# Experts' weights in tiles of 128 by 4096 (16 KB per partition) in five raw buffers, instead of tiles of 128 by 2048 in nine

## Chip, core and metric

The kernel runs on one core of a Trainium2 chip. The metric is device microseconds (us) of one execution, the median of several. Engines are named as the profile names them: PE is TensorE (PEld its weight load), DVE is VectorE, ACT is ScalarE, POOL is GpSimd, and SP is SyncE, which here issues almost all DMAs.

## What is computed

Two layers of a decoder trunk for 256 tokens of width 1024, in float32. Each layer has four token mixers, gates and an output projection, and then a feed-forward part: dense SwiGLU in layer 0, and in layer 1 eight experts, of which each token takes the best two. The change concerns the experts:

```python
def moe_swiglu(h, w_router, w1, w3, w2):        # w1, w3: 8 x 1024 x 3584, w2: 8 x 3584 x 1024
    logits = jnp.dot(t, w_router)
    top_val, top_idx = lax.top_k(logits, TOP_K)
    ...
    for e in range(N_EXPERTS):
        out = out + combine[:, e:e + 1] * swiglu(t, w1[e], w3[e], w2[e])
```

## The kernel before

**Weights.** All weights, 105 tiles of the mixers and the dense part and 336 of the experts, come from HBM in tiles of 1 MB, 128 partitions by 2048 floats. `load_raw` takes a buffer of 8 KB per partition, named `raw`, from a ring and issues the DMA on SP's queue; the ring is in the program's order, so a DMA waits on SP until the tile that had its buffer has been read for the last time, and all later DMAs wait behind it. In the front (mixers and dense part) the ring has four buffers (`rawp`); for the experts five more are put ahead of them (`rawm`), nine in all. `load_w` splits a tile for exact products: for each half of it, 1024 floats per partition, ACT copies it to `whi` (rounded, L165) and DVE computes `wlo = raw - whi` (L166). There are six pairs of `whi` and `wlo`. `mm3` makes a product from three matmuls: hi by hi (L157), hi by lo (L158), lo by hi (L159).

**Experts.** The eight experts are ordered by their tokens and paired: a large one with 128 slots, whose weights are split, and a small one with 64 slots, which reads `raw` itself with plain float32 matmuls, w1 on one half of PE's columns and w3 on the other. The 3584 hidden columns are done in seven chunks of 512, so there are 4 pairs x 7 = 28 steps. `paired` staggers them. In step s PE makes, in this order:

- `psu` of the large expert's chunk s (`up_large`, w1 and then w3: 48 matmuls), and between them `psT` (`turn_large`, four transposes);
- `psds`, the small expert's down projection of chunk s-2 (`down_small`: 16 matmuls straight from `raw`);
- `psq`, its up projection of chunk s-1 (`up_small`: 32 matmuls straight from `raw`), whose result ACT and DVE turn into `gfs` (L934, L935);
- `psd`, the large expert's down projection of chunk s-1 (`down_large`: 24 matmuls from split weights), and `psTs` (`turn_small`, four transposes of `gfs`).

So a step reads 12 tiles: w1, w1, w3, w3 of the large expert, w2, w2 of the small one, its w1, w3, w1, w3, and w2, w2 of the large one. At a change of pair PE also gathers the next pair's tokens (`psg`, `psgt`) and adds the results of the old one to the tokens (`pssc`).

The order on each engine is made by a scheduler when the program is built and is fixed after that. ACT and DVE work strictly in that order: an instruction that waits holds up all behind it.

Of the kernel before, what the change touches and what calls it, by code (L numbers as in the profile page):

```python
# [10 lines left out]
F32 = mybir.dt.float32  # L11
F32R = mybir.dt.float32r
# [5 lines left out]
P = 128  # L18
# [10 lines left out]
CONV_K = 31  # L29
WINDOWS = (2, 4, 8, 16)  # L30
NSLOT = 128
NRAW = 4
NRAW_MOE = 5
NSMALL = 64
RMS_EPS = 1e-6
LN_EPS = 1e-5
# [59 lines left out]
def decoder_kernel(ctx, tc, x_in, consts_in, mconsts_in, bias_in, small_in, gln_in, gbs_in, norms_in, w_in,  # L96
# [8 lines left out]
    psB = ctx.enter_context(tc.tile_pool(name="psB", bufs=4, space=bass.MemoryType.PSUM))  # L105


    ring = {"pools": [rawp] * NRAW, "i": 0, "skip": 0, "after": []}

    def hold_splits(ins, skip):  # L110

# [7 lines left out]
            yield  # L119

    def load_raw(src, a, n):
        pool = ring["pools"][ring["i"] % len(ring["pools"])]
        ring["i"] += 1
        raw = pool.tile([P, a, n], F32, name="raw", tag="raw")
        nc.sync.dma_start(raw, src)
        return raw

    def load_w(src, a, n):

        raw = load_raw(src, a, n)
        halves = []
        for i in range(2):
            r = raw[:, i * (a // 2):(i + 1) * (a // 2)]
            hi = wp.tile([P, a // 2, n], F32R, name="whi", tag="whi")
            lo = wp.tile([P, a // 2, n], F32R, name="wlo", tag="wlo")
# [4 lines left out]
        return halves, a // 2  # L142

    def wsl(wt, k, c0, n):
        halves, ah = wt
# [15 lines left out]
    def sl(pair, *idx):  # L161
        return (pair[0][idx], pair[1][idx])
# [505 lines left out]
    def moe(i, norm_i, l, mT):  # L668
        with ExitStack() as lctx:
# [6 lines left out]
            ring.update(pools=[rawm] * NRAW_MOE + [rawp] * NRAW, i=0)  # L676

            def small(shape, name, dt=F32):
                return wk.tile(shape, dt, name=name, tag=name, bufs=1)
# [129 lines left out]
            class Slots:  # L809
# [53 lines left out]

            line = {"last": []}

            def up_large(e, c, j0, xl):
                ps = psA.tile([P, 512], F32, name="psu", tag="mm")
                wt = [load_w(tile_of(e, c, j0 + j, 4), 4, 512) for j in range(2)]
                for k in range(KD):
                    last = mm3(ps, sl(xl, slice(None), k), wsl(wt[k // 4], k % 4, 0, 512), k == 0, k == KD - 1,  # L870
                               line["last"] if k == 0 else ())
                line["last"] = [last]
                return ps

            def gate_large(p1, p3):
                gf = wk.tile([P, 512], F32, name="gfm", tag="gf", bufs=2)
# [15 lines left out]
            def down_large(e, c, gT):  # L892
                if c == 0:
                    acc["l"] = [psB.tile([P, 512], F32, name=f"psd{n}", tag="ax") for n in range(2)]
                for j in range(2):
                    wt = load_w(tile_of(e, c, 4 + j, 2), 2, D)
                    for k in range(2):
                        for n in range(2):
                            last = mm3(acc["l"][n], sl(gT, slice(None), 2 * j + k), wsl(wt, k, n * 512, 512),
                                       c == 0 and j == 0 and k == 0, c == nch - 1 and j == 1 and k == 1,  # L900
                                       line["last"])
                            line["last"] = [last]

            def to_tokens(t, n, lhs, parts, w):
                ps = psA.tile([P, 512], F32, name="pssc", tag="mm")
# [15 lines left out]

            def up_small(e, c, xs):
                ps = psA.tile([P, 512], F32, name="psq", tag="mm")
                for j in range(2):
                    w1 = load_raw(tile_of(e, c, j, 4), 4, 512)
                    w3 = load_raw(tile_of(e, c, 2 + j, 4), 4, 512)
                    for k in range(4):
                        kk = 4 * j + k
                        for rows, w in ((LO, w1), (HI, w3)):
                            with behind(line["last"]):  # L930
                                line["last"] = [nc.tensor.matmul(ps[rows], lhsT=xs[:, kk], rhs=w[:, k], start=kk == 0,  # L931
                                                                 stop=kk == KD - 1)]
# [13 lines left out]
            def down_small(e, c, gT):  # L946
                if c == 0:
                    acc["s"] = psB.tile([P, 512], F32, name="psds", tag="ax")
                for j in range(2):
                    w = load_raw(tile_of(e, c, 4 + j, 2), 2, D)  # L950
                    for k in range(2):
                        for n, rows in enumerate((LO, HI)):
                            with behind(line["last"]):
                                line["last"] = [nc.tensor.matmul(  # L954
                                    acc["s"][rows], lhsT=gT[:, 2 * j + k], rhs=w[:, k, n * 512:(n + 1) * 512],
                                    start=c == 0 and j == 0 and k == 0, stop=c == nch - 1 and j == 1 and k == 1)]

            def scatter_small(GT, w):
                ys = wk.tile([P, 2, 512], F32R, name="ys", tag="ys", bufs=1)
# [5 lines left out]
            def paired():  # L965

                npair = NE // 2
                steps = npair * nch
                slots = {0: first}
                pend = gTs = None  # L970
                for s in range(steps + 1):
                    if s < steps:
                        pr, c = divmod(s, nch)
                        p1 = up_large(place_of[pr], c, 0, slots[pr].xl)
                    if pend is not None:
                        gT = turn_large(pend)
                    if s < steps:
                        gf = gate_large(p1, up_large(place_of[pr], c, 2, slots[pr].xl))
                        if c == nch - 1 and pr + 1 < npair:
                            nxt = slots[pr + 1] = Slots()  # L980
                            nxt.one_hot(None, posp[:, :, pr + 1:NE:npair])
                            nxt.inputs(0, NSLOT + NSMALL)
                            nxt.turned()
                    if s >= 2:
                        pr2, c2 = divmod(s - 2, nch)
                        down_small(place_of[npair + pr2], c2, gTs)
                        if c2 == nch - 1:
                            scatter_small(slots[pr2].GT, combp[:, :, npair + pr2:npair + pr2 + 1])
                    if s >= 1:
                        pr1, c1 = divmod(s - 1, nch)  # L990
                        gfs = up_small(place_of[npair + pr1], c1, slots[pr1].xs)
                        if s == steps:
                            sqrt_table(gfs[HI, 0:1], HI)
                        down_large(place_of[pr1], c1, gT)
                        if c1 == nch - 1:
                            scatter_large(slots[pr1].GT, combp[:, :, pr1:pr1 + 1])
                        gTs = turn_small(gfs)
                    pend = gf if s < steps else None
                down_small(place_of[NE - 1], nch - 1, gTs)
                scatter_small(slots[npair - 1].GT, combp[:, :, NE - 1:NE])  # L1000

            def rest(first_slot):
# [4 lines left out]
                for e in range(NE):  # L1007
# [4 lines left out]
                    sl_e.turned()  # L1012
                    for c in range(nch):
                        p1 = up_large(e, c, 0, sl_e.xl)
                        gT = turn_large(gate_large(p1, up_large(e, c, 2, sl_e.xl)))
                        down_large(e, c, gT)
                    scatter_large(sl_e.GT, comb[:, :, e:e + 1])

# [43 lines left out]
def layouts(inputs):  # L1062
# [5 lines left out]
    for l in range(L):  # L1068
# [13 lines left out]
    tiles = [f[k].reshape(M, NE, 2, 4, P, nch, 512).transpose(0, 1, 5, 2, 4, 3, 6).reshape(M, NE, nch, 2, P, 2048)  # L1082
             for k in ("moe_w1", "moe_w3")]
    tiles.append(f["moe_w2"].reshape(M, NE, nch, 2, 2, P, D).transpose(0, 1, 2, 3, 5, 4, 6)
                 .reshape(M, NE, nch, 2, P, 2048))
# [28 lines left out]
```

## Time and profile before

| | |
|---|---|
| median of 3 runs | 1543.84 us (1541.98 to 1545.42) |
| profiled execution | 1544.51 us, of which the span of the instructions is 1542.8 us |
| PE, DVE, ACT busy | 96%, 64%, 52% of the span |
| HBM read | 472.17 MB, 307 GB/s over the span |
| experts' part | from about 690 us to the end |

"Busy" of PE is modelled from overlapping matmuls, so a busy PE can still be a PE that is a little held up; how far apart matmuls start tells more. DMA share is the mean busy share of the 16 DMA engines. MB and GB/s are decimal, so a tile of 128 x 2048 floats is 1.05 MB.

### The profile page before, as it was taken

The numbers are of one execution on the slowest core, as the hardware profiler recorded it, in microseconds if no ns is written. First come the engines' busy times: TensorE is split into PE (matmuls) and PEld (weight loads), VectorE is DVE, ScalarE is ACT, GpSimd is POOL, SyncE is SP. The second block draws the span as 40 slices with busy tenths as digits, with TensorE's granted clock in tenths as the row PEclk, the third lists the DMA queues.
The fourth block names the chain that finished last, engine by engine and source line by source line (L and its number), as shares of the span: only waits on it lengthen the run. The fifth ranks groups of instructions, "written<-read, shape, count | busy, mean of one in ns | idle before, by whom it ended". The sixth has DMA issues, their size and how long they took to land.

```text
span 1542.8 us, 20057 instructions
## 1 busy us (share of the span) xinstructions
PE 1486.8 (96%) x7508; PEld 1072.2 (69%) x7508; DVE 979.9 (64%) x1291; ACT 809.6 (52%) x1184; POOL 20.3 (1%) x47
## 2 busy tenths in 40 slices
PE   6999998999989999989999999999999999899997
PEld 5888897888878888977566556656655665456553
DVE  5896776655668967756555565546654654556454
ACT  5567755555564777546454445435533553545343
POOL 2000000000000000000000000000000000000000
PEclk9999999999999999969999999999999999999998
DMA  9656455555555555639999999999999999999994
GB/s 333 192 178 201 162 191 170 191 188 186 178 193 178 177 181 164 265 125 383 385 421 421 421 394 420 421 421 421 421 405 421 421 421 421 375 397 421 421 421 199
DMA packets 134889, 474.61 MB, mean 308 GB/s; under 512 B 7744, under 2 KB 77376, under 8 KB 91776
## 3 DMA queue, kind: packets, MB, share of 16 engines
q1 hardware_dynamic: 132512, 466.65, 78.2%
q0 software_dynamic: 1984, 6.08, 1.2%
q8 instruction: 61, 1.00, 0.3%
q10 hardware_dynamic: 288, 0.52, 0.1%
q14 instruction: 44, 0.36, 0.1%
HBM read 472.17 MB, written 1.05 MB: 307 GB/s over the span
## 4 chain that ended last, share of the span: by engine, by line
PE 92%; DVE 4%; ACT 2%; issue 1%; DMA 1%; SPq 0%; DVEq 0%; ACTq 0%
PE psw L241 17%; PE psq L931 13%; PE psw L243 8%; PE psu L158 7%; PE psu L157 7%; PE psu L159 7%; PE psds L954 7%; PE psd L158 3%; PE psd L157 3%; PE psd L159 3%; DVE wlo L166 2%; PE psg L836 2%; PE psf L157 1%; PE psf L159 1%; PE psf L158 1%; PE psb L157 1%
## 5 line engine op out<-in xcount | busy, mean ns | idle before, releaser
L166 DVE TENSOR_TENSOR wlo<-raw,whi 128x1024 fp32r<-128x1024 f32 x546 | 648.3, 1222 | 242.0 <-ACT whi L165 237.9
L165 ACT ACTIVATE whi<-raw 128x1024 fp32r<-128x1024 f32 x546 | 554.6, 1054 | 272.8 <-DMA raw<-in_moe_w_dram 166.6
L241 PE MATMUL psw<-hp,whi 128*128 128x512 f32 x1088 | 388.7, 400 | 0.8 <-DVE hp L166 0.8
L243 PE MATMUL psw<-hp,wlo 128*128 128x256 f32 x1088 | 306.9, 282 | 0.0
L241 PEld LDWEIGHTS psw<-hp,whi 128*128 128x128 f32 x1088 | 205.0, 188 | 53.2 <-issue 3.3
L243 PEld LDWEIGHTS psw<-hp,wlo 128*128 128x128 f32 x1088 | 206.1, 189 | 2.1 <-issue 1.1
L931 PE MATMUL psq<-raw,xs 128*64 128x512 f32 x896 | 198.1, 593 | 1.8 <-DVE x L909 1.8
L157 PE MATMUL psu<-whi,xer 128*128 128x512 f32 x448 | 176.7, 394 | 3.2 <-DVE x L909 3.2
L158 PE MATMUL psu<-wlo,xer 128*128 128x512 f32 x448 | 177.8, 397 | 0.0
L159 PE MATMUL psu<-whi,xel 128*128 128x512 f32 x448 | 175.6, 392 | 0.0
L931 PEld LDWEIGHTS psq<-raw,xs 128*64 128x64 f32 x896 | 64.3, 137 | 129.0 <-issue 125.9
L954 PE MATMUL psds<-raw,gTs 128*64 128x512 f32 x448 | 103.6, 599 | 0.0
L157 PEld LDWEIGHTS psu<-whi,xer 128*128 128x128 f32 x448 | 84.8, 189 | 22.6 <-DVE x L909 4.5
L158 PEld LDWEIGHTS psu<-wlo,xer 128*128 128x128 f32 x448 | 84.8, 189 | 21.9 <-DVE wlo L166 3.7
L158 PE MATMUL psd<-wlo,gTr 128*128 128x512 f32 x224 | 92.2, 412 | 4.8 <-DVE wlo L166 4.8
L159 PEld LDWEIGHTS psu<-whi,xel 128*128 128x128 f32 x448 | 84.7, 189 | 16.9
L157 PE MATMUL psd<-whi,gTr 128*128 128x512 f32 x224 | 92.3, 412 | 2.7 <-ACT whi L165 2.7
L934 ACT ACTIVATE gfs<-psq 64x512 f32<-64x512 f32 x28 | 16.6, 591 | 143.2 <-PE psq L931 143.2
L935 DVE TENSOR_TENSOR gfs<-gfs,psq 64x512 f32<-64x512 f32 x28 | 19.4, 692 | 112.4 <-ACT gfs L934 112.4
L159 PE MATMUL psd<-whi,gTl 128*128 128x512 f32 x224 | 87.7, 391 | 0.0
L260 ACT ACTIVATE sum<-psw 128x256 f32<-128x256 f32 x120 | 44.8, 373 | 67.2 <-PE psw L243 67.2
L954 PEld LDWEIGHTS psds<-raw,gTs 128*64 128x64 f32 x448 | 29.8, 136 | 57.3 <-issue 56.3
(260 smaller groups left out, 1561.9 us busy)
## 6 DMA issues: line engine op xcount, KB each, us to landing
raw<-in_moe_w_dram SPq DMA_DIRECT2D x336, 1024.0 KB, 11.4
raw<-in_dense_w_dram SPq DMA_DIRECT2D x33, 1024.0 KB, 5.3
raw<-in_w_gate_dram SPq DMA_DIRECT2D x32, 1024.0 KB, 5.4
raw<-in_w_in_dram SPq DMA_DIRECT2D x22, 1024.0 KB, 5.5
raw<-in_w_out_dram SPq DMA_DIRECT2D x8, 1024.0 KB, 5.0
raw<-in_w_br_c_dram SPq DMA_DIRECT2D x4, 1024.0 KB, 5.3
s<-in_bias_dram POOLq DMA_DIRECT2D x16, 192.0 KB, 4.1
gain<-in_norms_dram SPq DMA_DIRECT2D x5, 512.0 KB, 4.6
```

The source lines that it names most:

```text
L157: nc.tensor.matmul(ps, lhsT=lhs[0], rhs=rhs[0], start=start, stop=False)
L158: nc.tensor.matmul(ps, lhsT=lhs[0], rhs=rhs[1], start=False, stop=False)
L159: return nc.tensor.matmul(ps, lhsT=lhs[1], rhs=rhs[0], start=False, stop=stop)
L165: return (nc.scalar.activation(hi, src, AF.Copy), nc.vector.tensor_tensor(out=lo, in0=src, in1=hi.bitcast(F32), op=ALU.subtract))
L166: nc.vector.tensor_tensor(out=lo, in0=src, in1=hi.bitcast(F32), op=ALU.subtract))
L241: nc.tensor.matmul(ps.rearrange("p a t -> p (a t)"), lhsT=w[0], rhs=act[:, k].rearrange("p a t -> p (a t)"), start=start, stop=False)
L243: nc.tensor.matmul(ps[:, 1], lhsT=w[1], rhs=act[:, k, 0], start=False, stop=stop)
L260: nc.scalar.activation(out[:, b], ps[b][:, 1], AF.Copy)
L836: nc.tensor.matmul(ps[:, b, cs], lhsT=ht[part][:, t, k * P:(k + 1) * P], rhs=self.G[:, t].rearrange("p s n -> p (s n)")[:, cs], start=n == ...
L931: line["last"] = [nc.tensor.matmul(ps[rows], lhsT=xs[:, kk], rhs=w[:, k], start=kk == 0, stop=kk == KD - 1)]
L935: nc.vector.tensor_tensor(out=gf[HI], in0=gf[HI], in1=ps[HI], op=ALU.mult)
L954: line["last"] = [nc.tensor.matmul(acc["s"][rows], lhsT=gT[:, 2 * j + k], rhs=w[:, k, n * 512:(n + 1) * 512], start=c == 0 and j == 0 and ...
```

## The change

A tile of the experts' weights becomes 128 partitions by 4096 floats, 2 MB, one run of 16 KB per partition, and the arrays are laid out so in HBM. A step reads six tiles instead of twelve. A raw buffer has 16 KB per partition; there are two in the front and three more for the experts, five in all (80 KB per partition instead of 72 KB). In the front two tiles of 1 MB share a buffer, one in each half, so a buffer is taken again when both have been read. `load_w` makes four splits of 1024 floats from a large tile. `up_small` waits for w1 and w3 whole. To make room, `gf` and `GT` have one buffer instead of two, and `turned` (the transposes `psgt` into `GT`) moves from the end of a pair to the third chunk of the next one.

```diff
-NRAW = 4
-NRAW_MOE = 5
+NRAW = 2
+NRAW_MOE = 3
...
     def load_raw(src, a, n):
-        pool = ring["pools"][ring["i"] % len(ring["pools"])]
-        ring["i"] += 1
-        raw = pool.tile([P, a, n], F32, name="raw", tag="raw")
+
+        if a * n > 2048 or ring["half"] is None:
+            pool = ring["pools"][ring["i"] % len(ring["pools"])]
+            ring["i"] += 1
+            raw = pool.tile([P, 4096], F32, name="raw", tag="raw")
+            ring["half"] = raw if a * n <= 2048 else None
+            raw = raw[:, 0:a * n]
+        else:
+            raw = ring["half"][:, 2048:4096]
+            ring["half"] = None
...
-        for i in range(2):
-            r = raw[:, i * (a // 2):(i + 1) * (a // 2)]
+        ah = 1024 // n
+        for i in range(a // ah):
+            r = raw[:, i * ah:(i + 1) * ah]
...
-                    self.GT = wk.tile([P, 2, TT, P], F32R, name="GT", tag="GT", bufs=2)
+                    self.GT = wk.tile([P, 2, TT, P], F32R, name="GT", tag="GT", bufs=1)
...
-                wt = [load_w(tile_of(e, c, j0 + j, 4), 4, 512) for j in range(2)]
+                wt = load_w(tile_of(e, c, j, KD), KD, 512)
...
-                for j in range(2):
-                    wt = load_w(tile_of(e, c, 4 + j, 2), 2, D)
...
+                wt = load_w(tile_of(e, c, 2, 4), 4, D)
...
-                for j in range(2):
-                    w1 = load_raw(tile_of(e, c, j, 4), 4, 512)
-                    w3 = load_raw(tile_of(e, c, 2 + j, 4), 4, 512)
...
+                w1, w3 = [load_raw(tile_of(e, c, j, KD), KD, 512) for j in range(2)]
...
+                    if s < steps and s > nch and c == 2:
+                        slots[pr].turned()
```

The scheduler orders the engines anew. In the front the orders of PE, ACT, DVE and POOL stay as they were; in the experts' part they don't. On ACT a step in the middle of the last pair (steps 24 and 25; `whi` is a split of the large expert's weights, `gfs` the small expert's activation, which waits for `psq`) stands before as:

```order
719 L165 ACTIVATE whi<-raw 128x1024 x3
720 L934 ACTIVATE gfs<-psq 64x512
721 L165 ACTIVATE whi<-raw 128x1024 x3
722 L943 ACTIVATE gTs<-psTs 128x256
723 L165 ACTIVATE whi<-raw 128x1024 x2
724 L165 ACTIVATE gTr<-psT 128x512
725 L165 ACTIVATE whi<-raw 128x1024 x4
726 L877 ACTIVATE gfm<-psu 128x512
```

Two of row 719's splits are still of the step's w3 and the third is the first quarter of the w2 that `psd` reads; its other three quarters are row 721, behind `gfs`. DVE's `wlo` and `gfs` stand in the same order. And of the change, the same part of the last pair:

```order
699 L174 ACTIVATE whi<-raw 128x1024 x4
700 L938 ACTIVATE gfs<-psq 64x512
701 L174 ACTIVATE whi<-raw 128x1024 x4
702 L947 ACTIVATE gTs<-psTs 128x256
703 L174 ACTIVATE whi<-raw 128x1024 x4
704 L174 ACTIVATE gTr<-psT 128x512
705 L886 ACTIVATE gfm<-psu 128x512
706 L174 ACTIVATE whi<-raw 128x1024 x4
707 L938 ACTIVATE gfs<-psq 64x512
```

All four quarters of w2 (rows 699 and 706) now stand ahead of `gfs`, and so they do in every step. On PE the next step (25), from `psds` on, reads before (`psd` has two accumulators, told apart by their numbers):

```order
5340 L954 MATMUL psds<-raw,gTs 64x512 x8
5341 L931 MATMUL psq<-raw,xs 64x512 x16
5342 L157 MATMUL psd_11115<-whi,gTr 128x512
5343 L158 MATMUL psd_11115<-wlo,gTr 128x512
5344 L159 MATMUL psd_11115<-whi,gTl 128x512
5345 L157 MATMUL psd_11116<-whi,gTr 128x512
5346 L158 MATMUL psd_11116<-wlo,gTr 128x512
5347 L159 MATMUL psd_11116<-whi,gTl 128x512
5348 L157 MATMUL psd_11115<-whi,gTr 128x512
5349 L941 MATMUL psTs<-ident,gfs 128x64 x4
5350 L158 MATMUL psd_11115<-wlo,gTr 128x512
5351 L159 MATMUL psd_11115<-whi,gTl 128x512
```

And the end of the 24 matmuls of `psd` in the change:

```order
5364 L167 MATMUL psd_10792<-wlo,gTr 128x512
5365 L168 MATMUL psd_10792<-whi,gTl 128x512
5366 L166 MATMUL psd_10793<-whi,gTr 128x512
5367 L167 MATMUL psd_10793<-wlo,gTr 128x512
5368 L168 MATMUL psd_10793<-whi,gTl 128x512
5369 L945 MATMUL psTs<-ident,gfs 128x64 x4
5370 L166 MATMUL psu<-whi,xer 128x512
5371 L167 MATMUL psu<-wlo,xer 128x512
```

`psTs` moved from behind the 7th matmul of `psd` (in other steps the 13th, in a few behind the 24th) to behind the 24th, in all steps but the first (where it stands there already, one matmul later).

## Rows read from the trace of the kernel before

**Rows 1.** Windows: share of time and rate, front, early and late experts
```profile
core 0: us, PE busy (x) PEld busy (x) DVE busy (x) ACT busy (x) POOL busy (x), PEclk, DMA share, GB/s
470.00:520.00 50.00, 50.00 (x292) 41.56 (x291) 47.30 (x94) 27.20 (x45) 0.00 (x0) 1.00 0.55 169
...
760.00:920.00 160.00, 156.17 (x720) 96.00 (x718) 87.91 (x89) 75.11 (x94) 0.00 (x0) 1.00 1.01 421
...
1360.00:1500.00 140.00, 137.68 (x619) 82.54 (x618) 71.10 (x68) 60.59 (x73) 0.00 (x0) 1.00 1.01 421
```

**Rows 2.** Chain that ended last, two early steps: start us, us, what
```profile
734.60 3.58 PE psds L954 x16
738.19 6.87 PE psq L931 x32
745.05 0.43 PE psd L157
...
750.72 0.23 PE psu L157
...
762.67 3.59 PE psds L954 x16
...
790.80 3.58 PE psds L954 x16
```

**Rows 3.** The same chain, late steps
```profile
1411.58 0.59 issue
1412.17 1.07 ACT whi L165
1413.26 1.24 DVE wlo L166
...
1430.35 3.58 PE psds L954 x16
...
1488.71 3.58 PE psds L954 x16
...
1506.83 3.58 PE psds L954 x16
...
1523.57 1.87 PE psds L954 x8
```

**Rows 4.** Timeline of ACT in a late step, with the idle time ahead
```profile
1435.19 1.06 ACT L165 ACTIVATE whi<-raw 128x1024 fp32r<-128x1024 f32 x1 [8.01 <-DMA raw<-in_moe_w_dram]
1440.88 0.59 ACT L934 ACTIVATE gfs<-psq 64x512 f32<-64x512 f32 x1 [4.63 <-PE psq L931]
1441.49 2.96 ACT L165 ACTIVATE whi<-raw 128x1024 fp32r<-128x1024 f32 x3
```

**Rows 5.** The same chain, around a change of pair
```profile
848.15 0.44 PE psgt L852 x4
...
851.11 1.76 PE psg L836 x16
...
881.25 3.58 PE psds L954 x16
...
945.25 3.58 PE psds L954 x16
```

**Rows 6.** DMA issues, 735 to 1507 us; issue to landing of all raw tiles
```profile
raw<-in_moe_w_dram SPq DMA_DIRECT2D x308, 1024.0 KB, 11.5
...
DMA to landing us min/median/max: 4.7/10.4/21.3
```

**Rows 7.** Timeline of ACT in the dense part; the dense tiles' DMA issues
```profile
299.98 1.06 ACT L165 ACTIVATE whi<-raw 128x1024 fp32r<-128x1024 f32 x1 [0.44 <-ACT sil L645]
301.39 1.06 ACT L165 ACTIVATE whi<-raw 128x1024 fp32r<-128x1024 f32 x1 [0.35 <-PE psw L241]
...
311.06 1.06 ACT L165 ACTIVATE whi<-raw 128x1024 fp32r<-128x1024 f32 x1 [0.85 <-PE psw L241]
...
raw<-in_dense_w_dram SPq DMA_DIRECT2D x33, 1024.0 KB, 5.3
```

More of the change, by code (lines that the diff above doesn't have):

```diff
@@ L105, in decoder_kernel @@
     psB = ctx.enter_context(tc.tile_pool(name="psB", bufs=4, space=bass.MemoryType.PSUM))
-    ring = {"pools": [rawp] * NRAW, "i": 0, "skip": 0, "after": []}
+    ring = {"pools": [rawp] * NRAW, "i": 0, "skip": 0, "after": [], "half": None}
     def hold_splits(ins, skip):
@@ L121, in load_raw @@
     def load_raw(src, a, n):
-        pool = ring["pools"][ring["i"] % len(ring["pools"])]
-        ring["i"] += 1
-        raw = pool.tile([P, a, n], F32, name="raw", tag="raw")
+        if a * n > 2048 or ring["half"] is None:
[7 more added lines that the diff above has]
+            ring["half"] = None
+        raw = raw.rearrange("p (a n) -> p a n", a=a)
         nc.sync.dma_start(raw, src)
@@ L133, in load_w @@
         halves = []
-        for i in range(2):
-            r = raw[:, i * (a // 2):(i + 1) * (a // 2)]
-            hi = wp.tile([P, a // 2, n], F32R, name="whi", tag="whi")
-            lo = wp.tile([P, a // 2, n], F32R, name="wlo", tag="wlo")
+        ah = 1024 // n
+        for i in range(a // ah):
+            r = raw[:, i * ah:(i + 1) * ah]
+            hi = wp.tile([P, ah, n], F32R, name="whi", tag="whi")
+            lo = wp.tile([P, ah, n], F32R, name="wlo", tag="wlo")
             with behind(ring["after"] if -6 < ring["skip"] <= 0 else []):
@@ L141, in load_w @@
             halves.append((hi, lo))
-        return halves, a // 2
+        return halves, ah
     def wsl(wt, k, c0, n):
@@ L675, in moe @@
             ps = out_proj(l, mT)
-            ring.update(pools=[rawm] * NRAW_MOE + [rawp] * NRAW, i=0)
+            ring.update(pools=[rawm] * NRAW_MOE + [rawp] * NRAW, i=0, half=None)
             def small(shape, name, dt=F32):
@@ L864, in moe, with up_large @@
             line = {"last": []}
-            def up_large(e, c, j0, xl):
+            def up_large(e, c, j, xl):
                 ps = psA.tile([P, 512], F32, name="psu", tag="mm")
-                wt = [load_w(tile_of(e, c, j0 + j, 4), 4, 512) for j in range(2)]
+                wt = load_w(tile_of(e, c, j, KD), KD, 512)
                 for k in range(KD):
-                    last = mm3(ps, sl(xl, slice(None), k), wsl(wt[k // 4], k % 4, 0, 512), k == 0, k == KD - 1,
+                    last = mm3(ps, sl(xl, slice(None), k), wsl(wt, k, 0, 512), k == 0, k == KD - 1,
                                line["last"] if k == 0 else ())
@@ L875, in gate_large @@
             def gate_large(p1, p3):
-                gf = wk.tile([P, 512], F32, name="gfm", tag="gf", bufs=2)
+                gf = wk.tile([P, 512], F32, name="gfm", tag="gf", bufs=1)
                 nc.scalar.activation(gf, p1, AF.Silu)
@@ L894, in down_large @@
                     acc["l"] = [psB.tile([P, 512], F32, name=f"psd{n}", tag="ax") for n in range(2)]
-                for j in range(2):
-                    wt = load_w(tile_of(e, c, 4 + j, 2), 2, D)
[L897 to L902, printed above, removed]
+                wt = load_w(tile_of(e, c, 2, 4), 4, D)
+                for k in range(4):
+                    for n in range(2):
+                        last = mm3(acc["l"][n], sl(gT, slice(None), k), wsl(wt, k, n * 512, 512),
+                                   c == 0 and k == 0, c == nch - 1 and k == 3, line["last"])
+                        line["last"] = [last]
             def to_tokens(t, n, lhs, parts, w):
@@ L923, in up_small @@
                 ps = psA.tile([P, 512], F32, name="psq", tag="mm")
-                for j in range(2):
-                    w1 = load_raw(tile_of(e, c, j, 4), 4, 512)
-                    w3 = load_raw(tile_of(e, c, 2 + j, 4), 4, 512)
[L927 to L932, printed above, removed]
+                w1, w3 = [load_raw(tile_of(e, c, j, KD), KD, 512) for j in range(2)]
+                for k in range(KD):
+                    for rows, w in ((LO, w1), (HI, w3)):
+                        with behind(line["last"]):
+                            line["last"] = [nc.tensor.matmul(ps[rows], lhsT=xs[:, k], rhs=w[:, k], start=k == 0,
+                                                             stop=k == KD - 1)]
                 gf = wk.tile([P, 512], F32, name="gfs", tag="gfs", bufs=1)
@@ L948, in down_small @@
                     acc["s"] = psB.tile([P, 512], F32, name="psds", tag="ax")
[L949 to L956, printed above, removed]
+                w = load_raw(tile_of(e, c, 2, 4), 4, D)
+                for k in range(4):
+                    for n, rows in enumerate((LO, HI)):
+                        with behind(line["last"]):
+                            line["last"] = [nc.tensor.matmul(
+                                acc["s"][rows], lhsT=gT[:, k], rhs=w[:, k, n * 512:(n + 1) * 512],
+                                start=c == 0 and k == 0, stop=c == nch - 1 and k == 3)]
             def scatter_small(GT, w):
@@ L977, in paired @@
                     if s < steps:
-                        gf = gate_large(p1, up_large(place_of[pr], c, 2, slots[pr].xl))
+                        gf = gate_large(p1, up_large(place_of[pr], c, 1, slots[pr].xl))
                         if c == nch - 1 and pr + 1 < npair:
@@ L982, in paired @@
                             nxt.inputs(0, NSLOT + NSMALL)
-                            nxt.turned()
                     if s >= 2:
@@ L1014, in rest @@
                         p1 = up_large(e, c, 0, sl_e.xl)
-                        gT = turn_large(gate_large(p1, up_large(e, c, 2, sl_e.xl)))
+                        gT = turn_large(gate_large(p1, up_large(e, c, 1, sl_e.xl)))
                         down_large(e, c, gT)
@@ L1081, in layouts @@
     M, nch = f["moe_w1"].shape[0], FE // 512
-    tiles = [f[k].reshape(M, NE, 2, 4, P, nch, 512).transpose(0, 1, 5, 2, 4, 3, 6).reshape(M, NE, nch, 2, P, 2048)
+    tiles = [f[k].reshape(M, NE, KD, P, nch, 512).transpose(0, 1, 4, 3, 2, 5).reshape(M, NE, nch, 1, P, 4096)
              for k in ("moe_w1", "moe_w3")]
-    tiles.append(f["moe_w2"].reshape(M, NE, nch, 2, 2, P, D).transpose(0, 1, 2, 3, 5, 4, 6)
-                 .reshape(M, NE, nch, 2, P, 2048))
+    tiles.append(f["moe_w2"].reshape(M, NE, nch, 4, P, D).transpose(0, 1, 2, 4, 3, 5).reshape(M, NE, nch, 1, P, 4096))
     moe_w = np.ascontiguousarray(np.concatenate(tiles, axis=3))
```

## The prediction

> **What bounds the kernel now.** I read the windows first, then the chain of work that ended last, then the timeline of ACT. The windows show two regimes [rows 1]. In the front PE is busy 50.00 us of 50 while the DMA engines are at 0.55: PE sets the time. In the experts' part both are near full: PE 156.17 of 160 us and the DMA share at 1.01 with 421 GB/s, which the last stretch repeats. So the chain has to say which of the two ends last there. It runs almost wholly through PE: `psds`, `psq`, `psd`, `psu`, and again. In the early steps nothing stands between: `psds` starts at 734.60, 762.67 and 790.80, so a step takes 28.1 us [rows 2]. In late steps it starts at 1430.35 and, two steps on, at 1488.71, so 29.2 us each, and between `psq` and the rest of `psd` the chain leaves PE: 0.59 us of issue, a `whi` of 1.07 and a `wlo` of 1.24 [rows 3].
>
> ACT's timeline says why. In a late step ACT makes one quarter of w2 at 1435.19 (it waited 8.01 us for the tile), then stands before `gfs`, which waits 4.63 us for the end of `psq`, and only from 1441.49 on makes the other quarters [rows 4]. The tile had been there; its splits were queued behind `gfs`, ahead of which `psd` could have had them. ACT's order in the kernel before shows the same: one quarter ahead of `gfs`, three behind it.
>
> How much is lost so: from 734.60 to 1488.71 are 25 steps in 754.1 us. At 28.1 they take 702.5. A change of pair adds 64.0 - 56.2 = 7.8 us in the two steps from 881.25 to 945.25, 32 `psg` at 0.11 (16 in 1.76) = 3.5, and `psgt` 0.44: 11.8 us, three times 35.3 [rows 2, 3, 5]. That leaves 754.1 - 702.5 - 35.3 = **16.3 us** of waits. The short step after (18.1 us to 1506.83, no `psu` in it) has about 1 more, as the one after it takes 16.7 to 1523.57 with the same work but four transposes.
>
> **The change, part by part.**
>
> *Order.* All four quarters of w2 come ahead of `gfs`, and `psTs` behind the whole of `psd`. If w2 lands in time, nothing stands between `psq` and `psd`, as in the early steps, where both w2 tiles happened to be split early: **-17.3 us**. If w2 is late, none of it is gained; so the bounds are 0 and -17.3, and I take the full amount and charge the lateness separately.
>
> *The transfers.* A 1 MB tile takes 1.049/0.421 = 2.49 us, two 4.98, and six pairs 29.9 us a step, against PE's 28.1. What a run of 16 KB costs no row shows. A 1 KB run takes an engine 0.55 x 16 x 1024/169 = 53 ns, an 8 KB run 1.01 x 16 x 8192/421 = 314 ns [rows 1]; a straight line through these has 16 ns that don't depend on length. An engine has 8 runs of 16 KB instead of 16 of 8 KB, so it saves between 0 and 8 x 16 = 0.13 us per 2 MB. I take the middle, 8 ns, since the 1 KB rows also hold waits that are no fixed cost: 4.92 us, 29.5 a step. [...]
>
> *The ring.* Count from the start of `psds`: `psq` ends at 10.5, `psd` at 16.1, the next `psds` starts at 28.1 [rows 2]. A tile's buffer is that of the fifth tile before it. The small expert's w2, w1 and w3 of the next step thus take the buffers of its w1 and w3 and of the large w2, free from 10.5 on. They move one after another: 10.5 + 3.0 + 3 x 4.92 = 28.3. The 3.0 is what a DMA takes beside the moving: at best 4.7 - 2.5 = 2.2 us [rows 6]; under load the median of 11.5 contains the queue and gives no number, so I take 3.0 and bound it by 2.2 and 4.4 (twice). `psq` needs w3 at 28.1 + 3.6 = 31.7, so 3.4 us are left. The large w2 follows at 33.2; four splits at 1.24 us, the first after 2.3, keep ahead of `psd`, which starts at 38.6. Before, `psq` could start on half of w1 and w3; this is the one place where the coarse tile costs something.
>
> With 29.5 against 28.1 the DMA falls back 1.4 us a step. Three of a pair's seven steps carry the change of pair, in which it catches up 11.8 us; in the other four it loses 5.7. That is 2.3 us more than the 3.4, waited for by `psq` in each of three pairs: **+6.9**. At the end there is no `psu` between the last two `psq`: 16.7 us of PE for four tiles, 19.7: **+2.9**.
>
> *`psgt`.* It now stands right behind `psTs`. With three of the four `psB` banks held by sums it must wait until ACT has copied `psTs` out: at least 0, at most one ACT instruction of 0.59 [rows 4] and some; I take 0.5, three times: **+1.5**. `gf` with one buffer costs nothing: its transposes stand on PE ahead of the matmuls that end in the next `gf`.
>
> *The front.* In the dense part a tile is used every 5.5 us (two from 299.98 to 311.06). The buffer is free when the second split's `wlo` is done, 301.39 + 1.06 + 1.24 = 303.7, the tile that takes it lands 5.3 later, at 309.0, and is first used four tiles on, at 322.1: 13 us ahead [rows 3, 7]. With halves, a tile waits for one more split, 5.5 us; 7.6 are left. I cost it at nothing; the cover is these 7.6 us, and if they were gone each pair of tiles would delay ACT's splits and then PE.
>
> *Sum*, on the profiled execution: 1544.5 - 17.3 + 6.9 + 2.9 + 1.5 = 1538.5. The median of the runs is 0.7 below that execution, so **1538 us**.
>
> **The rivals.**
>
> *The runs of 16 KB move no faster.* Then 4.98 us: 1.8 lost per step, 3 x (7.2 - 3.3) = 11.8, 3.2 at the end; -17.3 + 15.0 + 1.5 = -0.8, **1543 us**. For it speaks that 421 GB/s stands in every stretch as if capped [rows 1].
>
> *The fixed part is large.* 4.85 us: 1.0 lost per step, 3 x 0.4 + 2.7; -17.3 + 3.9 + 1.5 = -12, **1532 us**.
>
> *Slower: the ring of five starves PE.* If what a DMA takes beside the moving is 3.4 us more than I took, `psq` waits in every step outside a pair's change. Then a pair takes 42 x 4.92 = 206.6 plus the DMA's idling at the change, 11.8 - 4.2 = 7.6: 214.2 us against 754.1/25 x 7 = 211.1 now, 3.1 more, over 25 steps 11: **1555 us**. It decides from where the waits make up 15.8 us: 2 us less slack than I found. For it speaks that all five buffers are needed for tiles twice as long in coming; against it that in the late chain before, with twelve tiles a step, the waits lie behind `psq` and not ahead of it [rows 3]. [...]
>
> **How the numbers follow.** Forecast, 1534 to 1541: 0.42. Fixed part large, below 1534: 0.16. No faster runs, 1541 to 1547: 0.24. Starved, above 1547: 0.18. About 0.2%, 3.1 us, is what a measurement can tell from no change, so faster means below 1540.7: 0.58; within: 0.24; slower: 0.18. The range, 1530 to 1549, leaves out the end of the first rival of each side; the forecast's own is 1534 to 1541, from the 3.0 us at 2.2 (2.4 us better) and at 4.4 (4.2 worse).
>
> **What would show it.** Right: `psds` 28.1 us apart in steps without a pair's change; no `wlo` or `whi` in the chain between `psq` and `psd`; a rate near 426 GB/s; a wait of `psq` for w3 only late in a pair and at the end; the front's end unmoved. Wrong: `psq` waiting for a DMA in most steps, a rate below 421, `gfs` late because w2 is, or the first experts' matmuls starting later.

## The result, and the profile after

The change is faster: **1535.24 us** median (1531.68 to 1538.80) against 1544.18 of the kernel before in the same measurement, ratio 0.9944, 95% interval 0.9934 to 0.9953. The forecast was 1538 with a range of 1530 to 1549. One of the ten runs of the kernel before took 2475 us and is left out of the ratio. The profiled execution has a span of 1533.4 us, 9.4 less than before.

The windows of the changed kernel: the stretches of [rows 1], and the one between them.

```profile
core 0: us, PE busy (x) PEld busy (x) DVE busy (x) ACT busy (x) POOL busy (x), PEclk, DMA share, GB/s
470.00:520.00 50.00, 50.00 (x292) 41.55 (x291) 46.94 (x94) 26.13 (x42) 0.00 (x0) 1.00 0.54 172
760.00:920.00 160.00, 157.81 (x725) 98.50 (x725) 89.69 (x92) 74.99 (x94) 0.00 (x0) 1.00 1.01 428
920.00:1360.00 440.00, 435.19 (x1998) 272.23 (x1995) 257.65 (x257) 212.72 (x263) 0.00 (x0) 1.00 0.99 419
1360.00:1500.00 140.00, 138.72 (x622) 82.77 (x620) 70.47 (x67) 60.04 (x71) 0.00 (x0) 1.00 1.01 427
```

The front reads as before. Full stretches of the experts' part now move 427.5 GB/s instead of 421: a tile of 2.097 MB takes 4.905 us, two small ones took 4.98. But the middle stretch, which holds two changes of pair and what follows a third, has only 419: there DMA stands idle for a while, with a share of 0.97 from 920 to 960 us and 0.95 from 1120 to 1160 and from 1320 to 1360.

The chain that ended last, two early steps and part of a later one; it answers to [rows 2, 3].

```profile
734.71 3.58 PE psds L957 x16
738.29 6.87 PE psq L935 x32
745.16 0.43 PE psd L166
...
750.82 0.39 PE psTs L945 x4
...
754.38 0.45 PE psT L893 x4
754.88 0.47 issue
755.35 1.06 ACT whi L174
756.43 1.24 DVE wlo L175
757.71 0.50 PE psu L167
...
763.22 3.58 PE psds L957 x16
...
791.35 3.58 PE psds L957 x16
...
1462.16 18.64 DMA raw<-in_moe_w_dram
1480.80 0.04 issue
1480.84 7.09 PE psq L935 x30
...
1487.95 17.95 DMA raw<-in_moe_w_dram
1505.90 0.02 issue
1505.92 1.06 ACT whi L174
```

`psds` first starts at 734.71, as before (734.60): the front gave and took nothing. Between `psq` and `psd` the chain stays on PE, as forecast. But the steps are 28.5 and 28.1 us apart, because the pattern that was removed there has come back elsewhere: between `psT` and `psu` stand issue, a `whi` and a `wlo`. ACT's timeline shows it, with the idle time ahead in brackets:

```profile
1173.15 0.60 ACT L174 ACTIVATE gTr<-psT 128x512 fp32r<-128x512 f32 x1 [3.22 <-PE psT L893]
1173.65 3.89 ACT L174 ACTIVATE whi<-raw 128x1024 fp32r<-128x1024 f32 x4
...
1407.95 3.89 ACT L174 ACTIVATE whi<-raw 128x1024 fp32r<-128x1024 f32 x4
1411.74 0.59 ACT L174 ACTIVATE gTr<-psT 128x512 fp32r<-128x512 f32 x1
```

In the step at 1173 ACT waits 3.22 us before `gTr` for `psT`, and the four quarters of the large expert's w3 stand behind it; in the step at 1408 they stand ahead. The first kind is in ACT's order in eleven steps, and `psu` loses 0.45 us in ten of them; in the eleventh (step 13) the 16 `psg` stand between, and it loses nothing.

Late in each pair, and at the end, `psq` waits for tiles. From the waits, 735 us to the end (total, times, longest):

```profile
PEld psq L935 <- DMA raw<-in_moe_w_dram: 4.0, 5, 1.7
...
PE psq L935 <- DMA raw<-in_moe_w_dram: 0.8, 1, 0.8
```

**Where the time went.** The view of `psds` from 1470 to 1500 us (shortest, median and longest duration, first and last start) has the start of the 26th:

```profile
L957 PE MATMUL psds<-raw,gTs x32: 592/592/644, 1476.2 to 1498.2; 128*64 128x512 f32 x32
```

From the first, at 734.6, these 25 steps are 741.6 us against 754.1 before. Added up from each matmul's start to the next one's, by the tile that it writes, `psd` and `psTs` are 16.6 us shorter, `psu` is 6.0 longer, `psq` 2.2 longer, and `pssc` and `psT` together 4.1 shorter; the other tiles take as long as before. Of `psu`'s 6.0 the new stall has 10 x 0.45 = 4.5. `psq`, at its shortest 6.97 us from its first matmul to the next tile's, waits for tiles 0.58, 0.79, 0.50 and 0.33 us in four steps, 2.2. From the 26th `psds` to the end of the span it takes 57.2 us instead of 54.1: here `psq` waits 1.20 and 1.84 us for tiles.

### The profile page after: what moved, and what is told of

The parts are those of the page before. It is cut to its first block, busy times and chain, and to the rows that moved or that the text cites. A ratio compares the mean times of both kernels' runs of the same rounds, so it can differ in the third digit from the quotient of the medians.

```text
span 1533.4 us, 19285 instructions
## 1 busy us (share of the span) xinstructions
PE 1486.0 (97%) x7508; PEld 1079.7 (70%) x7508; DVE 977.0 (64%) x1291; ACT 808.9 (53%) x1184; POOL 20.3 (1%) x47
## 4 chain that ended last, share of the span: by engine, by line
PE 79%; DMA 12%; DVE 6%; ACT 2%; issue 1%; SPq 0%; DVEq 0%; ACTq 0%
PE psw L250 17%; DMA raw<-in_moe_w_dram 11%; PE psq L935 9%; PE psw L252 8%; PE psu L166 5%; PE psu L167 5%; DVE wlo L175 5%; PE psds L957 5%; PE psu L168 4%; PE psd L166 2%; PE psd L167 2%; PE psd L168 2%; PE psf L166 1%; PE psf L168 1%; PE psf L167 1%; PE psb L166 1%
## 5 line engine op out<-in xcount | busy, mean ns | idle before, releaser
L935 PE MATMUL psq<-raw,xs 128*64 128x512 f32 x896 | 202.4, 593 | 2.7 <-DVE x L916 1.8
L935 PEld LDWEIGHTS psq<-raw,xs 128*64 128x64 f32 x896 | 69.9, 137 | 128.7 <-issue 119.4
L167 PE MATMUL psd<-wlo,gTr 128*128 128x512 f32 x224 | 87.9, 392 | 0.4 <-DVE wlo L175 0.4
L887 DVE TENSOR_TENSOR gfm<-gfm,psu 128x512 f32<-128x512 f32 x28 | 19.2, 687 | 87.7 <-PE psu L168 87.7
L957 PEld LDWEIGHTS psds<-raw,gTs 128*64 128x64 f32 x448 | 29.9, 136 | 57.2 <-issue 56.9
L270 DVE TENSOR_TENSOR sum<-sum,psw 128x256 f32<-128x256 f32 x120 | 49.8, 415 | 23.1 <-ACT sum L269 23.0
```

What stands on the lines that cost most here:

```text
L167: nc.tensor.matmul(ps, lhsT=lhs[0], rhs=rhs[1], start=False, stop=False)
L270: nc.vector.tensor_tensor(out=out[:, b], in0=out[:, b], in1=ps[b][:, 0], op=ALU.add)
L935: line["last"] = [nc.tensor.matmul(ps[rows], lhsT=xs[:, k], rhs=w[:, k], start=k == 0, stop=k == KD - 1)]
L957: line["last"] = [nc.tensor.matmul(acc["s"][rows], lhsT=gT[:, k], rhs=w[:, k, n * 512:(n + 1) * 512], start=c == 0 and k == 0, stop=c == n ...
```

## The experiments

Two times of the profiled executions help to read them. One is the experts' part, from the first `psds` to the end of the span, since the front ends between 732.0 and 737.3 us whatever the kernel. The other is the time of a pair, from `psds` of the last step but one of the first pair to the same step of the last pair, a third of it; it is compared with what the tiles of a pair take at the rate of a full stretch, 42 of 4.905 us (206.0) or 84 of 2.49 (209.2). Where a kernel was run twice (changed and e8, e4 and e9, e6 and e10), the experts' part differs by 0.3 to 1.0 us. Each ratio is to the kernel before, timed beside the run (medians 1543.86 to 1545.15).

```
                                         median   ratio  95% interval    experts'   a pair   its tiles
before                                                                      808.3    213.2       209.2
changed                                 1535.24  0.9944  0.9934-0.9953      798.8    209.3       206.0
changed, again (e8)                     1534.93  0.9934  0.9922-0.9947      798.5    209.1       206.0
old order, large tiles (e1)             1560.11  1.0106  1.0091-1.0120      825.5    218.1       206.0
new order, small tiles (e2)             1537.35  0.9955  0.9941-0.9970      801.2    209.2       209.2
large tiles, runs of 8 KB (e3)          1545.72  1.0013  1.0004-1.0023      810.1    211.2       209.2
changed, w3 ahead of gTr (e4)           1536.36  0.9951  0.9938-0.9963      797.6    209.0       206.0
the same, again (e9)                    1534.71  0.9939  0.9927-0.9951      798.6    209.1       206.0
large buffers, halves of 8 KB (e5)      1538.31  0.9960  0.9948-0.9972      802.3    209.7       209.2
mixed tiles, w3 ahead of gTr (e6)       1524.04  0.9873  0.9859-0.9888      789.8    206.5       206.0
the same, again (e10)                   1524.26  0.9861  0.9847-0.9875      790.3    206.6       206.0
mixed tiles, gTr first in 11 (e7)       1535.82  0.9944  0.9931-0.9957      798.7    209.8       206.0
e7 with psT where the change has it (e11) 1527.87  0.9892  0.9876-0.9909    793.5    207.9       206.0
e6 with psT where the change has it (e12) 1525.27  0.9871  0.9855-0.9888    790.4    206.8       206.0
```

**Two theories.** The transfer theory: in both kernels the tiles pace a pair, and PE's own losses count only between a change of pair, where the tiles catch up, and the next wait for a tile; the time of a pair is its tiles plus the time that DMA idles at the change. The rival, the order theory (in later runs the PE theory), is the prediction's own sum: PE paces, each loss on it counts in full, and the gain is the order.

**e1, the old order with large tiles.**

```diff
-                nc.scalar.activation(gf[HI], ps[LO], AF.Silu)
-                nc.vector.tensor_tensor(out=gf[HI], in0=gf[HI], in1=ps[HI], op=ALU.mult)
+                hold_splits([nc.scalar.activation(gf[HI], ps[LO], AF.Silu),
+                             nc.vector.tensor_tensor(out=gf[HI], in0=gf[HI], in1=ps[HI], op=ALU.mult)], 1)
```

> The changed kernel, with three of the four quarters of w2 held behind gfs again, as in the kernel before; tiles, ring and layout as changed. Transfer theory (six tiles of 4.9 us pace the steps, and PE's own losses count only between a change of pair and the next wait of psq for a tile, some 3.5 steps of 7): 0.65 us lost per step in 12 or so of 27 steps, the rest taken out of waits for tiles: about 7 us over the changed kernel, 1540 to 1544. Order theory (the gain is the order, PE paces the steps): the whole 16.8 us that psd and psTs lost in the kernel before come back: 1550 to 1553. Third case, the order matters nothing: 1535.

Measured: 1560.11, worse than either. `psq` waits for no tile any more, a step without a change of pair takes 29.0 us (`psds` at 1198.04 and 1227.07), and the chain has the old stall:

```profile
1201.62 6.92 PE psq L935 x32
1208.57 0.59 ACT gfs L938
1209.18 1.07 ACT whi L174
1210.27 1.24 DVE wlo L175
```

In the kernel before, the early steps have all four quarters of w2 ahead of `gfs` and take 28.1 us [rows 2], and the late ones take 29.2; here every step has one. And of the 26.7 us by which the experts' part is longer than the changed kernel's, 17.2 arise in three steps, one at each change of pair (37.2, 37.3 and 36.8 us against 31.5, 30.5 and 32.1). There the forced order holds up more than `psd`: at the first, `yy` stands on DVE behind seven splits until 901.37 us and `psu` starts at 905.11 (in the change 899.05 and 901.14), with a mean granted clock of 0.57 from 905 to 910 us. So the run is a harder case than the old order, and its size can't be carried over. What it shows is that the order counts on large tiles too: the steps between are, but for one, 0.2 to 1.0 us longer than the changed kernel's.

**e2, the new order with the small tiles.** `gfs` is issued behind all splits of w2 on ACT and DVE; nothing else.

```diff
-                        gfs = up_small(place_of[npair + pr1], c1, slots[pr1].xs)
+                        pq = up_small(place_of[npair + pr1], c1, slots[pr1].xs)
+                        wt2 = down_w(place_of[pr1], c1)
+                        gfs = gate_small(pq, ring["made"])
...
-                        down_large(place_of[pr1], c1, gT)
+                        down_large(place_of[pr1], c1, gT, wt2)
...
+            def gate_small(ps, after):
                 gf = wk.tile([P, 512], F32, name="gfs", tag="gfs", bufs=1)
+                with behind(after):
...
```

> The kernel before, with all four quarters of w2 ahead of gfs in every step; tiles of 1 MB with runs of 8 KB, ring of nine, as before. Transfer theory: 84 tiles of 2.49 us are 209.2 us a pair and, with some 2 to 3 us of idle DMA at its change, as long as a pair takes now (211.1): what psd no longer loses, psq and psds wait for tiles: 1541 to 1546. Order theory: 1544.2 - 16.8, 1527 to 1530, and the large tiles of the change were a loss.

Measured: 1537.35, a miss for both. The first steps are 28.1 us apart (`psds` at 765.10 and 793.23), later ones wait for tiles as the transfer theory has it; but the experts' part is 7.1 us shorter, not nothing. The windows and waits say where the transfer theory's number was off, the kernel before first and this one below:

```profile
920.00:1360.00 440.00, 428.89 (x1954) 262.32 (x1955) 255.06 (x255) 208.42 (x258) 0.00 (x0) 1.00 0.99 411
```

```profile
920.00:1360.00 440.00, 433.88 (x1991) 269.68 (x1988) 259.71 (x257) 215.12 (x262) 0.00 (x0) 1.00 1.01 420
```

```profile
PEld psq L941 <- DMA raw<-in_moe_w_dram: 3.3, 4, 2.4
PE psq L941 <- DMA raw<-in_moe_w_dram: 1.5, 1, 1.5
```

I had left it 2 to 3 us of idle DMA at a change of pair, from the kernel before (411 GB/s through two changes). It has none: 420 GB/s, and a pair takes just its 84 tiles, 209.2. PE has losses of its own here, too (`psu` takes 5.6 us more than before), but they leave no DMA idle. The theory stands, with its idle time, put at 2 to 3 us in advance, found to be zero for nine small buffers once PE doesn't hold them. The order theory's 1527 to 1530 is out.

**e3, large tiles with runs of 8 KB.**

```diff
-        nc.sync.dma_start(raw, src)
+        if a * n > 2048:
+            h = a // 2
+            nc.sync.dma_start(raw[:, h:a], src[:, h:a])
+            nc.sync.dma_start(raw[:, 0:h], src[:, 0:h])
+        else:
+            nc.sync.dma_start(raw, src)
```

> The changed kernel, each 2 MB tile fetched by two DMAs with runs of 8 KB, the second half of the run first, so that whatever needs the first half still waits for the whole tile; buffers, ring, orders of PE and ACT nearly as changed. Run length theory: a tile takes 2 x 2.49 = 4.98 us again in place of 4.90, 42 tiles a pair 3.2 us more, three pairs and most of a fourth: about 11 us over the changed kernel, 1543 to 1548, and a rate of 421 GB/s in full stretches. If the rate came from the larger tile or the fewer DMAs waiting on a ring, and not from the run, it stays near 1535 and 427 GB/s.

Measured: 1545.72, as the run length theory has it. PE's order is that of the change but for the place of one `psT`.

```profile
920.00:1360.00 440.00, 432.94 (x1979) 270.62 (x1976) 254.86 (x255) 211.32 (x262) 0.00 (x0) 1.00 1.01 416
1360.00:1500.00 140.00, 138.86 (x617) 85.39 (x615) 72.96 (x70) 60.69 (x72) 0.00 (x0) 1.00 1.01 421
```

```profile
PEld psq L940 <- DMA raw<-in_moe_w_dram: 10.8, 7, 3.4
PE psq L940 <- DMA raw<-in_moe_w_dram: 4.6, 6, 2.5
```

The rate is 421 again, `psq`'s listed waits come to 15.4 us instead of 4.8 (those of PE lie inside those of PEld; from start to start `psq` is 7.5 longer), and the experts' part is 11.3 us longer than the changed kernel's. Besides the shorter runs this kernel has two DMAs to a tile. The packets in the traces tell the two apart: from 760 to 920 us a packet of 8 KB takes 314.5 ns in the kernel before and 314.3 here, one of 16 KB 615.9 in the change, 13 less than two; the packet of 4 bytes that each DMA adds on every engine takes 9. By these numbers an engine saves an estimated 8 x 13 = 104 ns per 2 MB by the longer run and 9 by having one DMA less. So the runs of 16 KB are worth nearly all of the 11.3 us. Read against e2, with the same order and the same runs, the large tiles cost 8.9.

**e4, w3 ahead of gTr in the changed kernel.** The load and splits of w3 are issued before `turn_large`, whose copies go behind them.

```diff
+                        wt3 = up_w(place_of[pr], c, 1)
...
-                        gT = turn_large(pend)
+                        gT = turn_large(pend, ring["made"] if s < steps else ())
...
-                split(gT[0], gT[1], ps)
+                with behind(after):
+                    split(gT[0], gT[1], ps)
```

> The changed kernel, with all four quarters of the large expert's w3 ahead of gTr on ACT and DVE in every step, which takes away the 0.45 us that psu loses after psT in ten or eleven steps. PE theory: all of it is gained, 4.7 us: 1530 to 1531. Transfer theory: only the stalls between a change of pair and the next wait for a tile count, one per pair, 1.4 us in all: 1533 to 1535, and psq waits longer for tiles by the rest.

Measured: 1536.36, above both ranges, and in e9, once more beside the changed kernel (e8):

> The changed kernel once more, unaltered, beside the others on the same chip: 1535, ratio 0.994.

> The changed kernel with w3 ahead of gTr once more, to narrow the interval: the transfer theory has 1.4 us less than the changed kernel on the same chip, the PE theory 4.7 less.

1534.71 against 1534.93. Added up from each matmul's start to the next one's, by tile, `psu` is 4.5 us shorter both times (280.8 and 280.9 against 285.3), and `psq` longer by 2.7 and 2.6 (197.1 and 197.0 against 194.4), with 0.3 to 0.6 each at `psT` and `psTs`. The experts' part is 1.2 us shorter in e4 than in the changed kernel and 0.1 longer in e9 than in e8, no difference that these runs can tell from none, nor from the transfer theory's 1.4. The PE theory's 4.7 is out; the transfer theory holds.

**e5, large buffers filled by halves.** Buffers and ring as changed, but runs of 8 KB, each half its own DMA, for the small expert in the order w1, w3, w1, w3; w2 held ahead of `gfs`.

```diff
-                w1, w3 = [load_raw(tile_of(e, c, j, KD), KD, 512) for j in range(2)]
+                w1, w3 = [load_raw(tile_of(e, c, j, KD), KD, 512, late=True) for j in range(2)]
+                for h in (slice(0, 4), slice(4, 8)):
+                    for j, w in enumerate((w1, w3)):
+                        nc.sync.dma_start(w[:, h], tile_of(e, c, j, KD)[:, h])
```

> The changed kernel's five buffers of 16 KB, each filled by two DMAs with runs of 8 KB, issued in the order of the kernel before (for the small expert the first halves of w1 and w3, then the second halves), so that psq starts on halves again and splits start on halves; all quarters of w2 ahead of gfs as in the change. It stands between two kernels already timed: the order alone with small tiles, 1537, and runs of 8 KB with waits for whole tiles, 1546. Wait theory (those 9 us are waits for whole tiles): back to 1536 to 1539, and the waits of psq for a DMA as short as with small tiles. Ring theory (they are buffers that come free only as a whole, so that DMA idles): 1543 to 1547.

Measured: 1538.31, the wait theory. The experts' part is 802.3, 1.1 from small tiles (e2) and 7.8 from waits for whole tiles (e3), and `psq`'s waits are short again:

```profile
PEld psq L950 <- DMA raw<-in_moe_w_dram: 3.8, 6, 2.1
PE psq L950 <- DMA raw<-in_moe_w_dram: 1.2, 1, 1.2
```

So of the 8.9 us that large tiles cost, 7.8 are waits for whole tiles; that five large buffers come free less often than nine small ones costs about 1.1, hardly more than two runs of one kernel differ.

**e6, long runs and short waits.** If so, tiles that keep the run of 16 KB, but of which `psq` needs only one to start, should have both gains. The small experts' w1 and w3 are read from a second layout, kept in HBM beside the first, in which one tile holds the first half of both and the next the second; `psTs` and the orders of e2 and e4 are forced.

```diff
-                w1, w3 = [load_raw(tile_of(e, c, j, KD), KD, 512) for j in range(2)]
-                for k in range(KD):
-                    for rows, w in ((LO, w1), (HI, w3)):
+                for j in range(2):
+                    w13 = load_raw(tile_of(e, c, 3 + j, KD), KD, 512)
+                    for k in range(4):
+                        kk = 4 * j + k
+                        for rows, o in ((LO, 0), (HI, 4)):
...
```

> The changed kernel with runs of 16 KB, but the small expert's w1 and w3 come from a second layout, in which a tile holds the same half of both: psq's first 16 matmuls need one tile, the other 16 the next, and the first buffer is free 3.5 us earlier. Order fixed on ACT and DVE: w2 ahead of gfs, w3 ahead of gTr; psTs behind psd. Wait theory: the waits of psq (6 us over the shortest, 188.2) go, and with DMA off the path the 4.8 us of psu that the order of w3 alone did not give count too: 1524 to 1527. Ring theory (a pair stays 206 us of tiles and 3.6 of idle DMA): 1532 to 1536.

Measured: 1524.04, and 1524.26 in e10.

> The mixed tiles with w3 first once more, beside the run with gTr first: 1524.

`psq` waits for no tile, the rate stays, and a pair takes 206.5 us, half a microsecond over its tiles:

```profile
920.00:1360.00 440.00, 437.19 (x2022) 273.82 (x2022) 257.81 (x257) 216.06 (x265) 0.00 (x0) 1.00 1.01 426
```

**e7, e11 and e12: which of its parts gave what.** e7 puts `gTr` ahead of w3 again in the eleven steps of the changed kernel.

```diff
+GTR_FIRST = (3, 5, 7, 10, 13, 14, 17, 18, 21, 24, 26)
...
+                        if s in GTR_FIRST:
+                            gT = turn_large(pend)
+                            hold_splits(ring["turned"], 0)
```

> The mixed tiles of the run before, with the large expert's w3 behind gTr again in the eleven steps in which the changed kernel has it so (3, 5, 7, 10, 13, 14, 17, 18, 21, 24, 26), and ahead of it in the others. It splits the gain of the mixed tiles from that of w3's order. PE theory (with no waits for tiles left, each 0.45 us counts): eleven times 0.45, 4.9 us more than with w3 always first, 1528 to 1530. Transfer theory (as in the changed kernel it is taken out of waits for tiles): 0 to 1.5 us more, 1524 to 1526.

Measured: 1535.82, 11.6 us worse than e10 beside it, more than either had. The scheduler had moved `psT` from behind the 13th matmul of `psu` to behind the 19th in five of these steps, so that `gTr` and the splits came later still (`gTr` at 1205.04 in the one below), and `psu` waited 1.8 us and more:

```profile
1204.57 0.45 PE psT L898 x4
1205.07 0.47 issue
1205.54 1.06 ACT whi L176
1206.62 1.24 DVE wlo L177
```

e11 and e12 hold `psT` behind the 13th matmul, with `gTr` first in the eleven steps and with w3 always first.

```diff
         with behind(after):
-            nc.tensor.matmul(ps, lhsT=lhs[0], rhs=rhs[0], start=start, stop=False)
-        nc.tensor.matmul(ps, lhsT=lhs[0], rhs=rhs[1], start=False, stop=False)
+            m = nc.tensor.matmul(ps, lhsT=lhs[0], rhs=rhs[0], start=start, stop=False)
+        with behind(mid(m) if mid else ()):
+            nc.tensor.matmul(ps, lhsT=lhs[0], rhs=rhs[1], start=False, stop=False)
```

> As the run with mixed tiles and gTr first in eleven steps (1535.8), but with psT held behind the 13th matmul of psu in every step, where it stands in the changed kernel; there it had slipped behind the 19th in five of the eleven, and psu waited 1.8 us and more in each. So this is the changed kernel with mixed tiles and nothing else of weight. PE theory: eleven times 0.45 over the run beside it (w3 always first), 4.9 us: 1528 to 1531, and the mixed tiles alone are worth some 5 us. If it stays at 1534 to 1536, the order of w3 and not the mixed tiles carried the gain, and what psq waited for was not what set the time; if it comes to 1524 to 1526, the eleven stalls are hidden.

> The same with w3 ahead of gTr in every step, psT behind the 13th matmul of psu: 1523 to 1526, as the mixed tiles with w3 first before.

Measured: 1527.87, 0.1 below the PE theory's range, and 1525.27. The mixed tiles alone are worth about 7 us over the changed kernel (5.0 to 5.3 in the experts' part), and the same order of w3 that gave nothing in e4 now gives 3.1 in the experts' part. `psu` is again 4.5 us shorter (ten steps, not the eleven of the expectations), and `psq` this time no longer (189.1 against 190.0); part goes at the end, where the last `psd` waits for w2 (8.3 us against 6.7). The intervals of the two ratios overlap, so the 3.1 rest on one profile each; e6 and e10, also with w3 always first, have 789.8 and 790.3 beside e12's 790.4.

## Why the prediction was right, point by point

*Order: right in size, wrong in what it is worth alone.* The prediction put the waits behind `gfs` in 25 steps at 16.3 us; `psd` and `psTs`, where they lay, are 16.6 shorter. That the two agree so well is partly luck: the account took 64.0 us for each change of pair, the third took 66.4 before, and the 2.4 too many went under these waits. Alone, with small tiles, the order gives 7.1 (e2), because the tiles set a pair to 209.2 us. The prediction charged the lateness of tiles in terms of its own, so its sum did not need the order to give as much alone.

*Transfers: right.* The forecast was 4.92 us per 2 MB and a rate near 426; 4.905 and 427.5 were measured, which is 9.4 ns saved per run of 16 KB ((4.98 - 4.905) / 8) where I took 8. e3 (421 GB/s with runs of 8 KB) and the packets (615.9 ns for 16 KB, 314.5 for 8 KB) show that it is the run length: the rival of runs that move no faster, priced at 1543, is e3's 1545.7.

*The ring's term was too large.* It had +6.9 for the waits in three pairs; they are 1.9, and 2.2 with the first wait of the last pair. Part of the difference is the new stall, which gave the tiles time: in e4, without it, the same waits are 3.8 (0.11, 1.34, 1.12, 0.03 and 1.19). For the rest the slack of 3.4 us at the start of a pair must have been put too small; that is inferred, and by how much was not measured. The tail: -1 + 2.9 in the sum, +3.1 measured.

*`psgt`: nothing measured,* where I took 1.5 of a range from 0; its three groups take 1.1 us in both kernels. *The front: nothing,* as forecast, so the 7.6 us of cover held.

*Two terms were not in the sum.* `psu` takes 6.0 us more. Of these 4.5 are the new stall, which e4 takes away; the other 1.5 are spread over the steps and were not traced. The order of the change shown ahead of the prediction is of a step in which w3 stands ahead of `gTr` (703 and 704 on ACT), and I had read only what stands around `gfs`. And `pssc` and `psT` take 4.1 less, at the changes of pair: before, `gTr` stood between the two `yy` on ACT, and `psT` ahead of the wait for them; now `psT` fills that wait between the `pssc`. All terms: -16.6 + 6.0 + 2.2 - 4.1 + 3.1 = -9.4, as measured, where the forecast was -6.0. So the sum is near because errors cancel, and that is luck: 6.0 left out at `psu` stands against 4.7 too much for the ring, 4.1 left out at the changes of pair and 1.5 for `psgt`.

*The rival of a starved ring* did not come, but what it names, `psq` waiting for tiles, is the largest cost of the change: whole tiles cost 8.9 us (e3 against e2), nearly all as waits (e5). e5 has the same two DMAs to a tile as e3 and gains 7.8 us at a DMA share of 1.01, since what reads a tile starts on its first half: `psq` waits 3.8 us for tiles (in PEld) instead of 10.8.

So the change is three things: order -7.1, whole tiles +8.9, long runs -11.3. That makes -9.5, the 808.3 - 798.8 of the experts' part; it must, since each run is compared with the next, and each price holds for its place in this row. How much the order is worth with large tiles was not settled: e1 overdoes the old one.

## What to carry to other kernels

Where a transfer and an engine are within a few per cent of each other (here, in a step, six tiles at 4.905 us, 29.4, and 28.1 of PE), price a step by the longer of the two over the whole cycle (here a pair: its tiles plus the idle DMA at its change), since here what one saved inside the cycle the other took back: in e4 `psu` was 4.5 us shorter and a pair took 209.0 us against 209.3, while the same edit gave 3.1 us in the experts' part once the other was out of the way (e12 against e11). Take long runs and short waits apart: a tile can be long in memory and still hold just what the next instructions need, as in e6 (426 GB/s, and `psq` waits for no tile). After a reordering, look for the removed pattern, a ready split queued behind an instruction that waits, at every other copy on the same engine (here `gTr`, 0.45 us in each of ten steps).

## What the runs showed of the hardware

Executions of kernels whose front has the same order reach the first `psds` at anything from 732.0 to 737.3 us. Part of that arises in the stretch behind the routing. From 660 to 680 us PE is busy 16.29 and 14.89 of the 20 us and the mean granted clock is 0.74 and 0.73; from 680 us on it comes back sooner or later (e6 first and e12 below):

```profile
660.00:680.00 20.00, 16.29 (x97) 14.85 (x94) 16.84 (x55) 7.06 (x14) 0.00 (x0) 0.74 0.27 91
680.00:700.00 20.00, 20.00 (x84) 17.00 (x84) 11.11 (x11) 12.87 (x15) 0.00 (x0) 0.83 0.75 284
```

```profile
660.00:680.00 20.00, 14.89 (x86) 12.94 (x86) 14.32 (x41) 7.14 (x17) 0.00 (x0) 0.73 0.10 34
680.00:700.00 20.00, 20.00 (x80) 17.57 (x80) 8.71 (x23) 11.01 (x16) 0.00 (x0) 0.67 0.69 267
```

With PE busy throughout, the stretch from 680 to 700 us had a mean granted clock of 0.83 in e6 (first `psds` at 732.0) and 0.67 in e12 (737.3); the changed kernel had 0.76 there (734.6). The traces have it at 0.50 of full speed from 669.7 to 686.8 us in e6, from 669.3 to 689.8 in the changed kernel and from 669.4 to 693.3 in e12. Of the 5.3 us between these two, 2.5 arise from the routing's first matmul (`pl`, at 658.7 and 661.5) to the first `psds`; 2.0 were there at the first `psw` (30.4 and 32.4), and 0.8 came in between, from causes that were not looked into. All of it lies ahead of the first `psds`, which is why the experts' part tells more than the median.
